# State products in rows of four, a contiguous tap table and whole-block turns in the S5 layer of a two-layer trunk on one Trainium2 core

## The chip, the core and the metric

The kernel runs on one core of one Trainium2 chip. A core has five engines that each work through their own queue of instructions in order: TensorE (PE: matmuls and transposes, with a separate queue PEld that loads the weights), VectorE (DVE), ScalarE (ACT), GpSimd (POOL) and SyncE (SP, which here starts all DMA transfers). They wait for each other only by semaphores. The metric is the device time of one execution in microseconds (us); of several executions the median counts, less is better.

## The reference

The model is a trunk of two layers on one sequence of 1024 steps with 1024 channels. Layer 0 is RWKV-7 time mixing, layer 1 an S5 state-space layer with a gated linear unit (GLU); each is followed by a squared-ReLU MLP, and every sub-layer by a layer norm of the scaled input plus the output. Only the S5 layer is changed. It has 64 groups of 16 channels; each group drives a diagonal complex state of 64 numbers.

```python
def s5_mix(x, a_re, a_im, log_dt, b_re, b_im, c_re, c_im, d_skip, w_glu):
    ...
    bbar_re, bbar_im = cmul(coef_re[..., None], coef_im[..., None], b_re, b_im)
    u = xf.reshape(bsz, n_chunks, CHUNK, SSM_GROUPS, SSM_GROUP).transpose(1, 2, 0, 3, 4)
    def chunk_step(h, u_c):
        bu_re = jnp.einsum('tbgc,gpc->tbgp', u_c, bbar_re)
        bu_im = jnp.einsum('tbgc,gpc->tbgp', u_c, bbar_im)
        pr, pi, sr, si = lax.associative_scan(combine, (a_ch_re, a_ch_im, bu_re, bu_im), axis=0)
        carry_re, carry_im = cmul(pr, pi, h_re[None], h_im[None])
        s_re, s_im = sr + carry_re, si + carry_im
        y = (jnp.einsum('tbgp,gcp->tbgc', s_re, cr_w) - jnp.einsum('tbgp,gcp->tbgc', s_im, ci_w))
        return (s_re[-1], s_im[-1]), y
    ...
    y = y.transpose(2, 0, 1, 3, 4).reshape(bsz, seq, d) + xf * d_skip
    y = jax.nn.gelu(y)
    z = y @ w_glu
    return z[..., :d] * jax.nn.sigmoid(z[..., d:])
```

## The kernel before

**Layout.** Activations lie with channels on the 128 partitions: `h[f]` is a tile of 128 channels (`f` from 0 to 7) by 512 steps, which is one half of the sequence. Half 0 is held in the tiles `hA`, half 1 in `hB`. The large products (MLP, GLU and the projections, called the bulk here) are made in three passes of rounded fp32 (`mm3`, all on line 188): every weight tile `wraw` is split into a rounded `whi` (ACT, L148) and a remainder `wlo` (DVE, L149), and one column of blocks sums into a PSUM bank `d`. `wload` (L169) is the DMA that fetches a weight tile. An instruction `L188 MATMUL d<-qbuf,whi` is one such bulk product.

**Order.** The tile framework schedules the instructions. Each has a rank; the bulk of the MLPs and the GLU has ranks from 200000 on, the S5 layer 99300 (half 0) and 99400 (half 1), its tables 99500, the layer norms 99000. A lower rank is taken first when its inputs are expected to be ready, and the bulk fills the places between; after this the order of each engine's queue is fixed in the program. So bulk products stand between the S5 layer's instructions on PE, and an S5 instruction that waits holds up the bulk behind it.

**PSUM.** Four pools share the eight banks: `d` (three, bulk), `l` (one, layer norms), `a` (two) and `c` (two).

**S5 tables** (L1105 to L1170, once). The layer works in blocks of `SL` = 8 steps, so 512 steps are `NSC` = 64 blocks. For each `f` (eight groups, two per `g2`: `par` is which of the two, in the partition halves) three tables are written to DRAM: `tB` (from inputs of a block to its states), `tC` (from states to outputs of a block) and `tT`, the taps, which take the inputs of a block straight to its outputs. For `tT` a product `pk` (L1151) gives the response to one input at distances of 0 to 7 steps, ACT copies it into `kpad` behind eight rows of zeros (cleared once by POOL), and two DMAs for each `f` (L1159) write eight shifted views of it as a block-Toeplitz table. In `kpad` and in `tT` the group `g` is the fastest index, so that the table of one group has every fourth element of a row.

**S5 layer**, once for each half (L1175 to L1268), with four rounds `f2` of two `f` each:

- Input: eight products with `ident` for each PSUM tile `pu1` turn 128 channels by every eighth step to 64 blocks by 128 channels (L154, L156: the upper partition half by a matmul, the lower by a transpose). ACT copies to `u1` (L1188). `pu2` (L1195) turns each group's part back, so that 8 steps x 16 channels lie on the partitions and the 64 blocks in the columns (`ug`, copied on L1197). `pbu` (L1206) multiplies with `tB`, and the result goes into the states `hb`.
- Scan: `advance` (L1216 to L1222) runs the recurrence over the 64 blocks, on DVE for groups of `g` 0 to 15 and on POOL for the rest, on DVE alone where the pieces are short.
- Output: for each `f2` the tables `tt` and `tcm` are loaded (L1240, L1242; tag `tab`, four buffers). For each `par` there is one PSUM bank `py`, into which 8 tap products (L1250, 128 partitions, `tt` streamed) and 16 state products (L1255, 64 partitions, `tcm` streamed) sum. ACT copies the bank to `y1` (L1257). Eight transposes for each `f` (`pyt`, L1263, in pool `a`) turn it back, DVE adds the direct path (`yg`, L1265, one buffer), ACT takes the GELU, and SP stores the row to DRAM as `s_y` (L1268), from where the GLU loads it as `yl` (L946).

## Time and profile before

| What | Value |
|---|---|
| median of 3 runs | 2742.12 us (2735.79 to 2742.68) |
| profiled execution, its time | 2746.6 us |
| span of its instructions | 2744.8 us |
| mean granted clock of TensorE | 0.961 |
| time busy: PE, PEld, DVE, ACT, POOL | 95%, 76%, 66%, 42%, 23% of the span |
| DMA | 345.90 MB, mean 126 GB/s |
| chain of work that ended last | PE 44%, DVE 4%, issue 3%, others 1% or less each |

The profile shows one execution. The span runs from the first to the last instruction; the execution's time is 1.8 us more. The times of the three runs lie within 6.9 us of each other, and the profiled execution lies 4.5 us above their median. A group such as `L1255 PE MATMUL py<-tcm,hb` is all instructions of one line and shape: their number, their busy time together, the mean duration of one, and the idle time before them. Durations of products that run beside each other overlap, so that a mean duration is not the time by which one of them delays the next.

### The profile page before, as it was taken

How to read it: one execution, taken by the hardware profiler on the slowest of the kernel's cores; microseconds unless marked ns; L12 is line 12 of the kernel's file. 1: busy time of each engine (PE TensorE's matmuls, PEld its weight loads, DVE VectorE, ACT ScalarE, POOL GpSimd, SP SyncE). 2: the span in 40 equal slices, each digit the busy share in tenths (PEclk: the TensorE clock that was granted, in tenths of full speed). 3: DMA queues.
4: the chain of work that ended last, by engine and by line, in shares of the span. 5: the costliest groups of instructions: out<-in, count | busy, mean ns of one | idle time of the engine just before them, and what ended most of it. 6: DMA issues, size and time to landing. Idle time of an engine off the chain costs nothing.

```text
span 2744.8 us, 43807 instructions
## 1 busy us (share of the span) xinstructions
PE 2598.4 (95%) x16582; PEld 2089.9 (76%) x16582; DVE 1813.3 (66%) x3191; ACT 1154.8 (42%) x2038; POOL 630.6 (23%) x515
## 2 busy tenths in 40 slices
PE   7999979989899999989999999999999999999997
PEld 5778757678677777767876788778778887788886
DVE  7477677577786867997567553674855546755556
ACT  7455574544543333353532332434223324433334
POOL 3121542432442122342122000120220101210101
PEclk9989979999899999999999999999999999999998
DMA  4765455564223334545333533233343322333333
GB/s 146 235 214 175 151 164 156 178 203 142 81 86 88 93 92 148 141 129 163 100 112 127 174 95 100 81 96 112 103 164 110 96 96 81 119 96 96 96 96 100
DMA packets 215058, 345.90 MB, mean 126 GB/s; under 512 B 21184, under 2 KB 75584, under 8 KB 214848
## 3 DMA queue, kind: packets, MB, share of 16 engines
q1 hardware_dynamic: 214848, 343.10, 40.5%
q8 instruction: 131, 2.15, 0.3%
q14 instruction: 79, 0.65, 0.1%
HBM read 279.06 MB, written 63.96 MB: 125 GB/s over the span
## 4 chain that ended last, share of the span: by engine, by line
PE 44%; DVE 4%; issue 3%; DMA 1%; POOL 1%; ACT 1%; ACTq 0%; SPq 0%; DVEq 0%; POOLq 0%
PE d L188 39%; PE py L1250 1%; PE py L1255 1%; DVE wlo L149 1%; DMA wraw<-in_mw_dram 1%; PE pu L154 1%; PE pbu L1206 1%; POOL rl L975 1%; DVE hA L991 0%; DMA s_y<-yg 0%; DVE t L1218 0%; DVE hB L991 0%; ACT whi L148 0%; DVE sq L876 0%; PE pu L1195 0%
## 5 line engine op out<-in xcount | busy, mean ns | idle before, releaser
L148 ACT CAST whi<-wraw 128x512 fp32r<-128x512 f32 x668 | 413.5, 620 | 929.1 <-PE d L188 623.2
L149 DVE TENSOR_TENSOR wlo<-wraw,whi 128x512 fp32r<-128x512 f32 x668 | 500.6, 750 | 426.8 <-ACT whi L148 404.3
L188 PE MATMUL d<-qbuf,whi 128*128 128x512 f32 (+1 forms) x2112 | 657.0, 394 | 23.8 <-DVE hA L991 12.8
L188 PEld LDWEIGHTS d<-qbuf,whi 128*128 128x128 f32 x2112 | 391.8, 191 | 120.0 <-DVE hA L991 17.8
L188 PE MATMUL d<-qbuf,wlo 128*128 128x512 f32 (+1 forms) x1056 | 411.9, 392 | 10.7 <-DVE wlo L149 10.4
L975 POOL TENSOR_TENSOR rl<-rl 128x512 f32<-128x512 f32 x128 | 157.2, 1228 | 1094.5 <-ACT rl L974 1094.5
L188 PE MATMUL d<-oAh,whi 128*128 128x512 f32 (+1 forms) x960 | 390.9, 411 | 15.5 <-ACT ev L418 6.3
L188 PE MATMUL d<-oAl,whi 128*128 128x512 f32 (+1 forms) x960 | 387.5, 405 | 3.0 <-DVE oAl L149 2.8
L188 PE MATMUL d<-oAh,wlo 128*128 128x512 f32 (+1 forms) x960 | 386.5, 405 | 2.4 <-DVE wlo L149 2.3
L188 PE MATMUL d<-oBh,whi 128*128 128x512 f32 x704 | 279.2, 397 | 0.0
L188 PE MATMUL d<-oBh,wlo 128*128 128x512 f32 x704 | 278.7, 396 | 0.2 <-DVE wlo L149 0.2
L188 PE MATMUL d<-oBl,whi 128*128 128x512 f32 x704 | 277.1, 394 | 0.0
L188 PEld LDWEIGHTS d<-qbuf,wlo 128*128 128x128 f32 x1056 | 201.7, 191 | 56.5 <-DVE wlo L149 14.5
L188 PEld LDWEIGHTS d<-oAh,whi 128*128 128x128 f32 (+1 forms) x960 | 185.9, 194 | 62.2 <-ACT ev L418 8.4
L188 PEld LDWEIGHTS d<-oAh,wlo 128*128 128x128 f32 (+1 forms) x960 | 185.8, 194 | 44.4 <-DVE wlo L149 3.2
L188 PEld LDWEIGHTS d<-oAl,whi 128*128 128x128 f32 (+1 forms) x960 | 185.6, 194 | 43.1 <-DVE oAl L149 5.2
L991 DVE TENSOR_TENSOR hB<-hB,d 128x512 f32<-128x512 f32 (+1 forms) x256 | 165.0, 650 | 71.2 <-PE d L188 68.0
L991 DVE TENSOR_TENSOR hA<-hA,d 128x512 f32<-128x512 f32 x240 | 162.1, 682 | 64.4 <-PE d L188 62.1
L188 PEld LDWEIGHTS d<-oBh,wlo 128*128 128x128 f32 x704 | 132.9, 189 | 32.4 <-issue 2.0
L188 PEld LDWEIGHTS d<-oBl,whi 128*128 128x128 f32 x704 | 133.1, 189 | 29.9 <-issue 0.7
L188 PEld LDWEIGHTS d<-oBh,whi 128*128 128x128 f32 x704 | 133.1, 189 | 29.0 <-issue 1.2
L149 DVE TENSOR_TENSOR qbuf<-rl,qbuf 128x512 fp32r<-128x512 f32 x128 | 95.0, 742 | 73.5 <-ACT qbuf L148 73.5
(374 smaller groups left out, 3804.8 us busy)
## 6 DMA issues: line engine op xcount, KB each, us to landing
wraw<-in_mw_dram SPq DMA_DIRECT2D x520, 256.0 KB, 2.7
wraw<-in_glu_dram SPq DMA_DIRECT2D x64, 256.0 KB, 2.7
low<-wlo SPq DMA_DIRECT2D x52, 256.0 KB, 2.6
wlo<-low SPq DMA_DIRECT2D x52, 256.0 KB, 3.6
wraw<-in_wk_dram SPq DMA_DIRECT2D x32, 256.0 KB, 3.5
wraw<-in_wr_dram SPq DMA_DIRECT2D x32, 256.0 KB, 3.9
wraw<-in_wv_dram SPq DMA_DIRECT2D x32, 256.0 KB, 4.3
yl<-s_y SPq DMA_DIRECT2D x32, 256.0 KB, 3.1
```

The costliest lines, as they stand in the source:

```text
L148: S.copy(hi, src)
L149: (e or V).tensor_sub(lo, src, hi.bitcast(F32))
L154: PE.matmul(out, x, idt, start=True, stop=True)
L188: bulk.append((PE.matmul(p, w, x, **kw).ins, x.shape[-1]))
L975: G.tensor_mul(r, r, r)
L991: V.tensor_add(z, z, p)
L1206: PE.matmul(p[qs, g2, ri], tb[:, g2, ri, qs], u[:, 2 * g2 + par], start=True, stop=True)
L1250: PE.matmul(p[64 * j : 64 * j + 64, g2], ug[f][:, 2 * g2 + par], tv[:, par, g2], start=g2 == 0, stop=False, skip_group_check=True)
L1255: PE.matmul(p[64 * j : 64 * j + 64, g2], hb[qs, 4 * f + g2, ri, 0:NSC], tcm[qs, g2, ri], start=False, stop=ri == 1, skip_group_check=True)
```

## The change

All of it is in the S5 layer and its tables. Line numbers of the kernel after are larger by 9 (bulk products: L188 becomes L197) to 19.

- **Input, turns of `h`.** In place of 64-row pieces of every eighth step, a whole 128x128 block is turned: all channels of one `f`, every fourth step (L1200). There are four for each `f`, all transposes. `u1` then has on its partitions 128 blocks of four steps.
- **Input, steps picked.** Blocks of four must be paired to blocks of eight. A new constant `sel` (made once, by one DVE copy of `ident` with even and odd columns apart) does it: `pu2` is now two products for each group (L1207), with the even and with the odd columns of `sel`, each into one half of the partitions.
- **Tap table.** `kpad`, `tT` and `tt` have the group ahead of the steps, so that one group's 128 numbers are contiguous. `kpad` is two tiles of four `f` each, of which POOL clears only the zeros; after every fourth `f`, 16 DMAs (two `par`, eight shifts) store four `f` at once, in place of two DMAs for each `f`.
- **Output.** Both banks `py` (one from pool `c`, one from pool `a`) are open at once. First all 16 tap products, then the 32 state products with the partition half (`par`, which is also the bank) as the innermost index and the column half (`j`) next. `inorder` ties each state product to the one ahead of it by a dependence without a semaphore, so that the scheduler keeps this order.
- **Turns of `y`.** `pyt` moves from pool `a` to the one bank of pool `l`.

```diff
+    sel = cp.tile([128, 2, 64], F32, name="sel")
+    V.tensor_copy(sel, ident.rearrange("p (n e) -> p e n", e=2))
...
+    def inorder(prods):
+
+        for x, y in zip(prods, prods[1:]):
+            tc.add_manual_dep(y.ins, x.ins.name, mybir.DependencyInfo(
+                mybir.DependencyClass.NoSync, mybir.DependencyReason.DATA), reason="order")
...
-    tT = dr.tile([KT, 128, 2, 512], F32, name="tT")
+    tT = dr.tile([128, 2, KT, 4, 128], F32, name="tT")
...
-        kpad = pp.tile([128, 16, 16, 4], F32, name="kpad")
-        G.memset(kpad, 0.0)
+        kpads = [pp.tile([128, TBF, 4, 16, 16], F32, name=f"kpad{j}") for j in range(KT // TBF)]
+        for kpad in kpads:
+            G.memset(kpad[:, :, :, 0:8], 0.0)
...
-                S.copy(kpad[ps_, 8:].rearrange("p t c g -> p g (t c)"), p[ps_])
-            tv = tT[f].rearrange("(s c) two n -> two c s n", c=16)
-            for par in range(2):
-                src = kpad[64 * par : 64 * par + 16, 1:9].rearrange("p t c g -> p (t c g)")
-                SP.dma_start(tv[par], bass.AP(src.tensor, src.offset, [src.ap[0], (64, SL), src.ap[1]]))
+                S.copy(kpad[ps_, f % TBF, :, 8:].rearrange("p g t c -> p g (t c)"), p[ps_])
+            if f % TBF == TBF - 1:
+                for par in range(2):
+                    for s in range(SL):
+                        SP.dma_start(
+                            tT[16 * s : 16 * s + 16, par, f - TBF + 1 : f + 1].rearrange("c f g n -> c (f g) n"),
+                            kpad[64 * par : 64 * par + 16, :, :, 1 + s : 9 + s].rearrange("c f g t e -> c (f g) (t e)"))
...
-            u1 = s5p.tile([128, 8, SL, 16], F32, tag="u1", name="u1", bufs=2)
-            for s2 in range(2):
+            u1 = s5p.tile([128, 2, 8, 4, 16], F32, tag="u1", name="u1", bufs=2)
+            for j in range(2):
                 p = pa.tile([128, 4, 128], F32, tag="a", name="pu1")
-                for j in range(2):
-                    src = h[2 * f2 + j].rearrange("p (c s) -> p c s", s=SL)
-                    for s in range(4):
-                        turn(p[64 * j : 64 * j + 64, s], src[:, :, SL - 1 - 4 * s2 - s], ident, j)
-                S.copy(u1[:, :, 4 * s2 : 4 * s2 + 4].rearrange("p g s c -> p s g c"),
-                       p.rearrange("p s (g c) -> p s g c", g=8))
+                src = h[2 * f2 + j].rearrange("p (m s) -> p s m", s=4)
+                for s in range(4):
+                    PE.transpose(p[:, s], src[:, 3 - s], ident)
+                S.copy(u1[:, j].rearrange("p g s c -> p s g c"), p.rearrange("p s (g c) -> p s g c", g=8))
...
                 for g in range(8):
-                    PE.transpose(p[:, g], u1[ps_, g].rearrange("p s c -> p (s c)"), ident[ps_, ps_])
+                    for e in range(2):
+                        PE.matmul(p[64 * (1 - e) : 64 * (1 - e) + 64, g], u1[:, j, g].rearrange("p s c -> p (s c)"),
+                                  sel[:, e], start=True, stop=True)
...
-                tabs.append((f, tt.rearrange("p two (n g) -> p two g n", g=4), tcm))
+                tabs.append((f, tt.rearrange("p two (g n) -> p two g n", g=4), tcm))
+            pp = [r.tile([128, HT], F32, tag=t, name="py").rearrange("p (g n) -> p g n", g=4)
+                  for r, t in ((pc, "c"), (pa, "a"))]
+            for g2 in range(4):
+                for par in range(2):
+                    for j, (f, tv, tcm) in enumerate(tabs):
+                        PE.matmul(pp[par][64 * j : 64 * j + 64, g2], ug[f][:, 2 * g2 + par], tv[:, par, g2],
+                                  start=g2 == 0, stop=False, skip_group_check=True)
+            prods = []
+            for g2 in range(4):
+                for ri in range(2):
+                    for j, (f, tv, tcm) in enumerate(tabs):
+                        for par in range(2):
+                            qs = slice(64 * par, 64 * par + 64)
+                            prods.append(PE.matmul(pp[par][64 * j : 64 * j + 64, g2], hb[qs, 4 * f + g2, ri, 0:NSC],
+                                                   tcm[qs, g2, ri], start=False, stop=ri == 1, skip_group_check=True))
+            inorder(prods)
             for par in range(2):
-                qs = slice(64 * par, 64 * par + 64)
-                p = pc.tile([128, HT], F32, tag="c", name="py").rearrange("p (g n) -> p g n", g=4)
...
-                S.copy(y1[:, :, :, par].rearrange("p t g c -> p g t c"), p.rearrange("p g (t c) -> p g t c", t=SL))
+                S.copy(y1[:, :, :, par].rearrange("p t g c -> p g t c"), pp[par].rearrange("p g (t c) -> p g t c", t=SL))
...
-                p = pa.tile([128, SL, NSC], F32, tag="a", name="pyt")
+                p = pl.tile([128, HT], F32, tag="l", name="pyt").rearrange("p (t n) -> p t n", t=SL)
```

Two places of PE's queue show what moved. The first is the turning of the input in half 0, round `f2` = 2, in the kernel before: L156 and L154 are turns of `hA` into a bank `pu1`, and the rows `d` are bulk products. Each row gives the line, the operation, output and inputs with the number of the buffer, the shape, and a count where instructions of one kind follow each other.

```order
L156 MATMUL pu1_13604<-ident_84,hA_7672 64x128 x4
L154 MATMUL pu1_13604<-ident_84,hA_7712 64x128 x4
L188 MATMUL d_14659<-oBh_12101,whi_14662 128x512
L188 MATMUL d_14659<-oBl_12102,whi_14662 128x512
L188 MATMUL d_14659<-oBh_12101,wlo_14663 128x512
L188 MATMUL d_14659<-oBh_12107,whi_14662 128x512
L188 MATMUL d_14659<-oBl_12108,whi_14662 128x512
L156 MATMUL pu1_13614<-ident_84,hA_7672 64x128 x4
L154 MATMUL pu1_13614<-ident_84,hA_7712 64x128 x4
```

The same place in the kernel after, from the second bank of that round on: L1200 is a whole-block turn, L1207 the picking of steps with `sel`.

```order
L1200 MATMUL pu1_13646<-ident_84,hA_7714 128x128 x4
L197 MATMUL d_14695<-qbuf_9518,whi_14691 128x512 x2
L197 MATMUL d_14695<-qbuf_9518,wlo_14692 128x512
L197 MATMUL d_14695<-qbuf_9518,whi_14691 128x512 x2
L197 MATMUL d_14695<-qbuf_9518,wlo_14692 128x512
L1207 MATMUL pu2_13652<-sel_112,u1_13639 64x64 x16
L1207 MATMUL pu2_13691<-sel_112,u1_13639 64x64 x16
```

A bank holds four turns of 128x128 from one `f` in place of eight of 64x128 from two, and the picking has 16 products of 64 columns for each `f` behind it, with other bulk products between.

The second place is the output stage of half 0, with the turns of `y` of round `f2` = 0 and the products of round 1. In the kernel before (names without the buffer's number, so that products into one bank stand in one row):

```order
L188 MATMUL d<-qbuf,wlo 128x512
L1250 MATMUL py<-tt,ug 64x128
L1263 MATMUL pyt<-ident,y_13883 128x64 x16
L1250 MATMUL py<-tt,ug 64x128 x7
L1255 MATMUL py<-tcm,hb 64x128 x16
L1250 MATMUL py<-tt,ug 64x128 x8
L1255 MATMUL py<-tcm,hb 64x128 x16
L188 MATMUL d<-oBh,whi 128x512
```

And in the kernel after, where L1282 is the turns of `y`, L1264 the tap products and L1272 the state products:

```order
L197 MATMUL d<-qbuf,wlo 128x512
L1282 MATMUL pyt<-ident,y_13935 128x64 x8
L1264 MATMUL py<-tt,ug 64x128 x14
L1272 MATMUL py<-tcm,hb 64x128 x13
L1282 MATMUL pyt<-ident,y_13935 128x64 x8
L1272 MATMUL py<-tcm,hb 64x128 x19
L1264 MATMUL py<-tt,ug 64x128 x2
L197 MATMUL d<-qbuf,whi 128x512 x2
```

The second eight turns of `y` now stand behind 14 tap and 13 state products, and behind the last state products stand the first two tap products of the next round, ahead of the bulk.

More of the change, by code (lines that the diff above doesn't have):

```diff
@@ L33 @@
 TB = 2
+TBF = 4
 LN8R = 400000
```

13 lines of the change are left out of this document (2 added, 11 removed).

## The prediction

> **What bounds the kernel now.** I read the page first, then the busy time by stage, then the timeline of TensorE inside the stages that the change touches.
>
> ```profile
> span 2744.8 us, 43807 instructions
> PE 2598.4 (95%) x16582; PEld 2089.9 (76%) x16582; DVE 1813.3 (66%) x3191; ACT 1154.8 (42%) x2038; POOL 630.6 (23%) x515
> ...
> L149 DVE TENSOR_TENSOR wlo<-wraw,whi 128x512 fp32r<-128x512 f32 x668 | 500.6, 750 | 426.8 <-ACT whi L148 404.3
> ```
>
> TensorE (PE) is busy for 95% of the span, so its time counts, but only where it is also the last to wait. The busy time by stretch shows that (columns: stretch, its length, busy time and instruction count of PE, PEld, DVE, ACT, POOL, granted clock, DMA share, GB/s).
>
> ```profile
> 1327.00:1400.00 73.00, 73.00 (x577) 59.23 (x577) 33.80 (x52) 32.07 (x55) 4.18 (x4) 1.00 0.33 105
> 1400.00:1480.00 80.00, 72.35 (x354) 55.24 (x351) 68.18 (x115) 21.23 (x36) 25.95 (x14) 0.97 0.32 99
> 1480.00:1542.00 62.00, 62.00 (x534) 46.95 (x533) 28.82 (x39) 21.88 (x36) 8.68 (x5) 0.99 0.63 219
> ...
> 1940.00:2010.00 70.00, 62.67 (x257) 47.86 (x254) 65.90 (x112) 18.82 (x32) 18.08 (x10) 0.96 0.27 87
> 2010.00:2071.00 61.00, 61.00 (x532) 46.76 (x532) 27.66 (x36) 20.41 (x35) 7.49 (x5) 0.99 0.55 190
> 1072.00:1270.00 198.00, 178.08 (x931) 135.86 (x931) 184.06 (x355) 85.85 (x136) 70.50 (x50) 0.95 0.54 149
> ```
>
> The S5 layer has three stages in each half: the input is turned (1327 to 1400 in half 0), the scan runs on DVE (1400 to 1480), the outputs are made (1480 to 1542). In the first and the third PE is busy for 73.00 of 73 and 62.00 of 62 us, and DVE for less than half: a microsecond of PE saved there is saved. In the scan, and while the tables are made (1072 to 1270), DVE is nearly full (68.18 of 80, 184.06 of 198) and PE has idle time already.
>
> **The change part by part.** Counts first. An fp32 product shows as two records, a transpose as one; the rows are of half 0 for hA (hB has the same again) and of both halves for the others.
>
> ```profile
> L1250 PE MATMUL py<-tt,ug 128*64 128x128 f32 x256 | 40.4, 408 | 0.0
> ...
> L1255 PE MATMUL py<-tcm,hb 64*64 64x128 f32 x512 | 32.5, 275 | 0.0
> ...
> L154 PE MATMUL pu<-ident,hA 128*64 128x128 f32 x64 | 9.5, 294 | 0.0
> ...
> L1195 PE MATMUL pu<-ident,u 64*128 64x64 f32 x128 | 8.1, 229 | 0.0
> ...
> L156 PE MATMUL pu<-ident,hA 128*64 128x128 f32 x32 | 4.6, 272 | 0.0
> ```
>
> Records overlap, so I take their price from start to start in the timeline of PE (columns: start, length of the run, what, how many). First the turning stage:
>
> ```profile
> 1327.37 1.03 PE L156 MATMUL pu<-ident,hA 128*64 128x128 f32 x8
> 1328.34 2.19 PE L154 MATMUL pu<-ident,hA 128*64 128x128 f32 x16
> 1330.46 0.73 PE L188 MATMUL d<-qbuf,whi 128*128 128x512 f32 x2
> ...
> 1337.99 1.01 PE L1195 MATMUL pu<-ident,u 64*128 64x64 f32 x16
> 1338.94 0.50 PE L188 MATMUL d<-oBh,wlo 128*128 128x512 f32 x1
> ...
> 1343.73 2.09 PE L1206 MATMUL pbu<-ug,tb 128*64 128x64 f32 x64
> 1345.74 0.50 PE L188 MATMUL d<-oBl,whi 128*128 128x512 f32 x1
> ```
>
> *Turning h.* Eight L156 records take 0.97 us to the next start, 0.121 each; sixteen L154 records take 2.12, 0.133 each. So 64 x 0.121 + 128 x 0.133 = 24.8 us. After it there are 64 transposes of whole 128x128 blocks, all of the one-record kind; at 0.121 they cost 7.7. **Gain 17.1.** Their weights, 128 columns taken from every fourth element of h, are not in this trace. L156 reads every eighth and L154, at 0.133, the same; twice L156's price (0.242) is my upper end, 7.7 us more. I take 0.121, since it is the nearest row.
>
> The SBUF — State Buffer page of the Trainium skill (Specifications (TRN2)) says that a read at full bandwidth needs two hits in each 16-byte line and that each new line pays; every fourth fp32 is a new line each time, so by it the new turns pay and the forecast would be some 7 us later. L156, whose step also leaves the line each time, ran at 0.121 us, so I don't count it.
>
> *Picking the steps.* 128 transposes at 0.95 / 16 = 0.059 cost 7.6 us. They become 256 products with `sel`, of the form of L1206 (128 rows, 64 columns of weights, 64 columns streamed, column halves in turn): 2.01 / 64 = 0.0314 a record, 512 records, 16.1 us. **Loss 8.5.**
>
> Now the output stage, one f2 of it:
>
> ```profile
> 1489.03 0.65 PE L1250 MATMUL py<-tt,ug 128*64 128x128 f32 x2
> 1489.60 1.01 PE L1263 MATMUL pyt<-ident,y 64*128 64x64 f32 x16
> 1490.55 2.01 PE L1250 MATMUL py<-tt,ug 128*64 128x128 f32 x14
> 1492.49 1.96 PE L1255 MATMUL py<-tcm,hb 64*64 64x128 f32 x32
> 1494.38 2.01 PE L1250 MATMUL py<-tt,ug 128*64 128x128 f32 x16
> 1496.33 1.96 PE L1255 MATMUL py<-tcm,hb 64*64 64x128 f32 x32
> 1498.22 0.51 PE L188 MATMUL d<-oBh,whi 128*128 128x512 f32 x1
> ```
>
> *Tap products.* 32 L1250 records take 0.57 + 1.94 + 1.95 = 4.46 us, 0.139 each, 35.6 for 256. State products stream 128 columns as well and take 1.89 / 32 = 0.059. The difference is the streamed table, which steps over four elements; another product with 128 contiguous columns, pk, runs as the state products do:
>
> ```profile
> 1125.14 1.71 PE L1151 MATMUL pk<-ca,bb 64*16 64x128 f32 x28
> ```
>
> 28 records in 1.71 us, 0.061 with the last one's drain. At 0.059 the 256 tap records cost 15.1. **Gain 20.5.** If the step was not the cause, the gain is 0; nothing else differs from L1206 but the width.
>
> *State products.* 512 x 0.059 = 30.2 us, two side by side (two column halves). Four in a row use both row halves too, into two banks. The trace has this once by chance, where the first half's 32 records of a run of 64 end and the second's begin. Instructions in flight at four moments, by short stretches on that line (PE's count is the first in brackets):
>
> ```profile
> 1482.30:1482.31 0.01, 0.01 (x5) 0.01 (x2) 1.00 1.05 410
> ...
> 1483.06:1483.07 0.01, 0.01 (x10) 0.01 (x4) 1.00 0.00 0
> 1484.00:1484.01 0.01, 0.01 (x5) 0.01 (x2) 1.00 0.00 0
> ```
>
> Ten records are in flight instead of five: four run at once at the pace of two. So 30.2 becomes 15.1: **gain 15.1.** The turns of y are cut into 16 pieces in place of 8 and the products are cut at them; at about 0.1 us a piece (an estimate from the gaps between the rows above) that is a loss of 0.8.
>
> On PE: 17.1 - 8.5 + 20.5 + 15.1 - 0.8 = 43 us.
>
> *What comes late next.* Three rows on the y's, from DVE's timeline, and two landings:
>
> ```profile
> 1494.35 1.19 DVE L1265 SCALAR_TENSOR_TENSOR yg<-hA,pv,pyt 128x512 f32<-128x512 f32 x1 [2.82 <-DMA s_y<-yg]
> 1504.58 1.19 DVE L1265 SCALAR_TENSOR_TENSOR yg<-hA,pv,pyt 128x512 f32<-128x512 f32 x1 [2.17 <-PE pyt L1263]
> 1508.62 1.16 DVE L1265 SCALAR_TENSOR_TENSOR yg<-hA,pv,pyt 128x512 f32<-128x512 f32 x1 [0.86 <-DMA s_y<-yg]
> ```
>
> ```profile
> tt<-tT SPq DMA_DIRECT2D x16, 512.0 KB, 4.2
> ...
> s_y<-yg SPq DMA_DIRECT2D x16, 256.0 KB, 2.8
> ```
>
> One f2 took PE 9.2 us of products plus 21 bulk products at 0.23, 14 us. It becomes 1.0 (turns) + 1.9 + 1.9 + 0.5 and 18 bulk at 0.23, about 9.4. But yg has one buffer: the next y waits for the store of the last (4.0 us from 1504.58 to 1508.62, more where the store is slow), two of them 8 to 12 us. pyt moves into the ring "l", which has one bank: the second turn waits for DVE to finish the first y, and PE, which is in order, with all bulk behind it, waits too. Also two tap products of the next f2 now stand before the bulk (below the 19 state products). Their table's buffer is freed by the tap products of this f2, 32 state products and a turn earlier, 2.5 us, and the load takes 4.2: a wait of about 2 us at four places. I give back 12 us in all (8 of it by these four waits, the rest by the turns); the bounds are 0, if stores land in 2 us and waits overlap, and 6 f2 x 3.3 = 20.
>
> In the scans the order has 28 more bulk products than before (288 and 280 for 270 each). DVE is full there, and each twelve bring one wlo (0.75 us) and about one add more: I count 3 us back, 0 to 5.
>
> At nothing: in the table stage `kpad` is cleared and stored in two blocks of 16 DMAs (POOL has 128 of 198 us free; ACT's sixteen copies of 1.07 us get cheaper, off the path). Each block keeps SP for about 16 x 0.36 = 6 us without a weight load, and SP has slack there, since it waits for DVE:
>
> ```profile
> SPq L169 <- DVE wlo L149: 100.0, 48, 7.9
> ```
>
> If that cover is gone, two blocks cost up to 12. The copy of `sel` at the start is below 0.3.
>
> **The sum** is 43 - 12 - 3 = 28 us off the profiled execution (span 2744.8, run 2746.6), so 2718.6; the runs' median, 2742.12, lies 4.5 lower: **2714**.
>
> **The rivals.** (1) *Nothing is given back*: y's stores land in 2 us and no table is late. 2742 - 43 = 2699. For it: DVE is under half busy there. Against it: the wait for s_y is in the rows. (2) *The output stage keeps its length*, held by tables, stores and the single bank: then only the turning stage (8.6) and the tap products ahead of the scan (a quarter of 20.5, 5) are won, 2728. For it: DMA is at 0.63 there and must carry the same bytes in two thirds of the time. (3) *Four in a row run two at a time*: the change doesn't do what it says, 15 us less, and the waits shrink by about 5 since PE comes later: 2724. For it: each product is two records for one part of the array, and if a record that waits for its part stops all behind it, no more than two overlap. Against it: the ten in flight. The page TensorE: Matmul & The Clock Gate of the Trainium skill (Part 3, The mechanism) calls the matmuls' start strictly first in, first out, which would give this rival; the trace disagrees with it at 1483.06. (4) *Slower by the clock*:
>
> ```profile
> 1470.00:1475.00 5.00, 1.93 (x6) 0.97 (x6) 5.00 (x6) 1.05 (x2) 1.15 (x1) 0.99 0.11 13
> 1475.00:1481.00 6.00, 5.20 (x12) 3.80 (x12) 6.00 (x8) 1.24 (x2) 4.01 (x3) 0.50 0.20 77
> ```
>
> After 5 us with PE busy for 1.93, the clock was granted at 0.50 for 6 us, which costs 3. If the new waits (16 turns of y and 4 tables, 2 us each) trip it too, each costs 5: nine use the gain up, eleven of the twenty give 2742 - 43 + 55 = 2754. Against it: waits of 2 us leave PE mostly busy in any 5.
>
> **How the numbers follow.** Chances: the forecast 0.60 (its own range 2704 to 2725), (1) 0.14, (2) 0.14, (3) 0.08, (4) 0.04. The range of 2696 to 2734 takes in all but (4) and the outer ends of (1) and (2), which move by the bounds above (the turns up to 7.7 dearer, the return of waits from 0 to 20), about 0.8. 0.3% is 8.2 us, about what a measurement of this kernel can tell from no change: faster than 2734 is all of the forecast, (1) and (3) and some four in ten of (2), 0.88; the rest of (2) lies within, 0.08; slower is (4), 0.04.
>
> **What would show it.** Right: tap records in pairs at 0.109 us from pair to pair, state records four to 0.109 us, 64 whole turns at 0.12, the step products at 0.031; the output stages at about 46 us each with PE idle for some 6 in each, before pyt and the first tap products. Wrong: state records still at 0.059; whole turns above 0.2; output stages at 60 us; half-clock rows in the output stages; or PE idle in the table stage by 10 us more, beside the two blocks of stores.

## The result and the profile after

The change made the kernel slower: 2754.41 us median of 9 runs (2744.84 to 2760.1) beside 2737.66 us of 9 runs of the kernel before (2726.34 to 2749.15); the ratio is 1.0056, 95% interval 1.0038 to 1.0074. That is some 15 us in the wrong direction; the forecast had been 28 us less. (The ratio of the run called sel alone below leaves out one of its twelve executions, which took 5681.63 us.) The page of the profiled execution, in the rows that answer to those of before (the split of the weights, L148 and L149 before, is L151 and L152 here):

```profile
span 2758.1 us, 44305 instructions
PE 2574.1 (93%) x16838; PEld 2080.2 (75%) x16838; DVE 1824.3 (66%) x3192; ACT 1146.2 (42%) x2038; POOL 627.2 (23%) x516
...
L152 DVE TENSOR_TENSOR wlo<-wraw,whi 128x512 fp32r<-128x512 f32 x668 | 505.2, 757 | 408.9 <-ACT whi L151 390.2
```

PE is busy for 24 us less and the span is 13 us longer, so PE waits for some 38 us more. Where, is best seen between marks that stand at the same work in both kernels. Both issue the same 9338 bulk records (products into `d`) in nearly the same order, so I take the times at which the 3181st, 3841st, 4561st, 5881st and 6481st begin. They bound the table stage, the S5 layer of half 0, a stretch without S5 work, and the S5 layer of half 1 (us, each from one profiled execution; the first mark is at 1071.6 us before and 1081.7 after):

| | tables | S5, half 0 | between | S5, half 1 | the four |
|---|---|---|---|---|---|
| before | 214.3 | 250.3 | 310.3 | 218.5 | 993.4 |
| after | 238.8 | 234.8 | 311.1 | 212.2 | 997.0 |

The S5 layer gained 21.8 us and **the table stage lost 24.5**. The busy time of the table stage, from its first mark to its last, before and then after (columns as in the prediction):

```profile
1071.60:1285.90 214.30, 194.38 (x1005) 149.37 (x1004) 194.69 (x372) 89.39 (x142) 72.82 (x52) 0.95 0.56 157
```

```profile
1081.70:1320.50 238.80, 197.04 (x1005) 150.91 (x1004) 196.31 (x372) 81.78 (x142) 73.31 (x53) 0.90 0.51 141
```

The work is the same (1005 products, 372 and 372 DVE instructions, DVE 195 and 196 us); the stage has only become longer around it, at a lower granted clock. What stood in the way is in SP's timeline: start, length, how many. First the change, with the weight loads (L172) and the table load `bc` (L1121) around its first block, then three of the eight pairs of stores of before:

```profile
1181.06 0.33 SPq L172 DMA_DIRECT2D wraw<-in_mw_dram  x1
1181.44 19.54 SPq L1170 DMA_DIRECT2D tT<-kpad  x16
...
1204.41 0.82 SPq L1121 DMA_DIRECT2D bc<-in_s5bc_dram  x1
1205.29 11.48 SPq L172 DMA_DIRECT2D wraw<-in_mw_dram  x4
...
1285.55 20.28 SPq L1170 DMA_DIRECT2D tT<-kpad  x16
```

```profile
1128.61 0.90 SPq L1159 DMA_DIRECT2D tT<-kpad  x2
...
1158.20 2.37 SPq L1159 DMA_DIRECT2D tT<-kpad  x2
...
1268.48 0.86 SPq L1159 DMA_DIRECT2D tT<-kpad  x2
```

A block of 16 stores of the tap table holds SP for 20 us, 1.25 us a store on the mean, and no weight load leaves in that time; the next one starts 23.8 and 21.7 us after the block's start. The stretches behind the two blocks, and what PE waited for from the first mark to 1345 us (us, times, longest; 26.6 us of it lie in the table stage, where the kernel before has no such wait over 0.15 us):

```profile
1201.00:1209.00 8.00, 0.00 (x0) 0.00 (x0) 0.00 (x0) 1.08 (x2) 0.00 (x0) 0.74 0.89 226
1290.00:1306.00 16.00, 8.26 (x37) 6.46 (x35) 4.23 (x7) 0.68 (x2) 0.00 (x0) 0.83 0.76 99
1306.00:1322.00 16.00, 7.54 (x24) 5.77 (x24) 5.29 (x9) 1.78 (x3) 2.56 (x2) 0.64 0.77 245
```

```profile
PE d L197 <- ACT whi L151: 27.5, 4, 15.3
```

For 8 us behind the first block no matmul ran; behind the second PE stood for half of 32 us, and the clock fell to 0.64. The chain goes from the store over SP's queue to the weight load, `whi`, and the bulk product. The tables' own transfers were held too: DVE stood for 8.4 us until 1209.04 for the load `bc` that SP could start only at 1204.41.

In the S5 layer the trace shows most of what was forecast. The timeline of PE, from a turn of `h` to the picking of steps and then one output round:

```profile
1364.64 1.12 PE L1200 MATMUL pu<-ident,hA 128*128 128x128 f32 x8
...
1371.86 0.86 PE L1207 MATMUL pu<-sel,u 128*64 128x64 f32 x22
...
1498.60 1.98 PE L1272 MATMUL py<-tcm,hb 64*64 64x128 f32 x64
1500.51 0.50 PE L197 MATMUL d<-oBh,whi 128*128 128x512 f32 x1
...
1506.21 0.71 PE L1282 MATMUL pyt<-ident,y 64*128 64x64 f32 x8
1506.84 1.96 PE L1264 MATMUL py<-tt,ug 128*64 128x128 f32 x28
1508.73 1.08 PE L1272 MATMUL py<-tcm,hb 64*64 64x128 f32 x26
1509.75 0.71 PE L1282 MATMUL pyt<-ident,y 64*128 64x64 f32 x8
1510.39 1.32 PE L1272 MATMUL py<-tcm,hb 64*64 64x128 f32 x38
1513.14 0.65 PE L1264 MATMUL py<-tt,ug 128*64 128x128 f32 x4 [1.43 <-DMA tt<-tT]
```

64 state records take 1.91 us, 0.030 each, where before 32 took 1.89: four in a row do run at once. 28 tap records take 1.89, 0.068 each in place of 0.139. At 1513.14 stands the forecast wait for a tap table, 1.43 us.

### The profile page after: what moved, and what is told of

Read it like the earlier page. It is cut to its first block, busy times and chain, and to the rows that moved or that the text cites. A ratio compares the mean times of both kernels' runs of the same rounds, so it can differ in the third digit from the quotient of the medians.

```text
span 2758.1 us, 44305 instructions
## 1 busy us (share of the span) xinstructions
PE 2574.1 (93%) x16838; PEld 2080.2 (75%) x16838; DVE 1824.3 (66%) x3192; ACT 1146.2 (42%) x2038; POOL 627.2 (23%) x516
## 4 chain that ended last, share of the span: by engine, by line
PE 63%; DVE 16%; DMA 8%; ACT 5%; issue 4%; POOL 2%; SPq 2%; ACTq 0%; DVEq 0%; POOLq 0%
PE d L197 54%; DVE wlo L152 3%; PE pA L605 2%; SPq L1170 1%; DMA wraw<-in_wr_dram 1%; ACT whi L151 1%; DMA wraw<-in_mw_dram 1%; DMA tt<-tT 1%; DMA s_r<-ev 1%; DVE t L1231 1%; DMA ldsg<-s_sg 1%; DVE hA L1000 1%; PE pu L1207 1%; PE pbu L1219 1%; DVE qbuf L152 1%
## 5 line engine op out<-in xcount | busy, mean ns | idle before, releaser
L151 ACT CAST whi<-wraw 128x512 fp32r<-128x512 f32 x668 | 413.8, 620 | 963.6 <-PE d L197 635.7
L152 DVE TENSOR_TENSOR wlo<-wraw,whi 128x512 fp32r<-128x512 f32 x668 | 505.2, 757 | 408.9 <-ACT whi L151 390.2
L197 PE MATMUL d<-qbuf,whi 128*128 128x512 f32 (+1 forms) x2112 | 660.8, 396 | 41.1 <-ACT whi L151 16.3
L197 PEld LDWEIGHTS d<-qbuf,whi 128*128 128x128 f32 x2112 | 395.2, 192 | 136.2 <-DVE hA L1000 22.4
L197 PE MATMUL d<-qbuf,wlo 128*128 128x512 f32 (+1 forms) x1056 | 413.4, 394 | 9.2 <-DVE wlo L152 9.0
L197 PE MATMUL d<-oAh,whi 128*128 128x512 f32 (+1 forms) x960 | 393.0, 412 | 28.6 <-ACT whi L151 10.6
L984 POOL TENSOR_TENSOR rl<-rl 128x512 f32<-128x512 f32 x128 | 148.9, 1163 | 1084.2 <-ACT rl L983 1084.1
L197 PE MATMUL d<-oAl,whi 128*128 128x512 f32 (+1 forms) x960 | 388.9, 406 | 2.5 <-DVE oAl L152 2.4
L197 PE MATMUL d<-oAh,wlo 128*128 128x512 f32 (+1 forms) x960 | 387.1, 406 | 1.3 <-DVE wlo L152 1.3
L197 PE MATMUL d<-oBh,whi 128*128 128x512 f32 x704 | 279.4, 397 | 3.2 <-DVE hB L1000 1.9
L197 PE MATMUL d<-oBh,wlo 128*128 128x512 f32 x704 | 278.3, 396 | 0.0
L197 PE MATMUL d<-oBl,whi 128*128 128x512 f32 x704 | 277.0, 393 | 0.0
L197 PEld LDWEIGHTS d<-qbuf,wlo 128*128 128x128 f32 x1056 | 202.8, 192 | 55.5 <-DVE wlo L152 13.1
L197 PEld LDWEIGHTS d<-oAh,whi 128*128 128x128 f32 (+1 forms) x960 | 186.7, 195 | 73.8 <-ACT whi L151 11.1
L197 PEld LDWEIGHTS d<-oAl,whi 128*128 128x128 f32 (+1 forms) x960 | 187.0, 195 | 43.0 <-DVE oAl L152 4.6
L197 PEld LDWEIGHTS d<-oAh,wlo 128*128 128x128 f32 (+1 forms) x960 | 186.6, 195 | 43.4 <-DVE wlo L152 2.1
L197 PEld LDWEIGHTS d<-oBh,whi 128*128 128x128 f32 x704 | 133.1, 189 | 31.9 <-issue 3.1
L197 PEld LDWEIGHTS d<-oBh,wlo 128*128 128x128 f32 x704 | 132.7, 189 | 32.0 <-issue 1.8
L197 PEld LDWEIGHTS d<-oBl,whi 128*128 128x128 f32 x704 | 132.9, 189 | 29.9 <-issue 1.0
L152 DVE TENSOR_TENSOR qbuf<-rl,qbuf 128x512 fp32r<-128x512 f32 x128 | 99.9, 780 | 66.3 <-ACT qbuf L151 66.1
```

The source lines that it names most:

```text
L151: S.copy(hi, src)
L152: (e or V).tensor_sub(lo, src, hi.bitcast(F32))
L197: bulk.append((PE.matmul(p, w, x, **kw).ins, x.shape[-1]))
L984: G.tensor_mul(r, r, r)
```

## The experiments

The table gives for each run the ratio to before with its interval, and the same four stretches from its one profiled execution. One execution says little about a few us: sel alone, which changes next to nothing, differs from before by 6 us in the sum, and it is the timed ratio that decides.

| run | ratio (95%) | tables | S5, 0 | S5, 1 | the four |
|---|---|---|---|---|---|
| the change | 1.0056 (1.0038 to 1.0074) | 238.8 | 234.8 | 212.2 | 997.0 |
| old tap table | 0.9976 (0.9961 to 0.9991) | 213.6 | 244.3 | 219.1 | 987.4 |
| new tap table alone | 1.0066 (1.0049 to 1.0083) | 235.8 | 244.0 | 211.2 | 1002.6 |
| sel alone | 1.0012 (0.9998 to 1.0025) | 210.9 | 248.8 | 217.7 | 987.3 |
| 16 small stores after each f | 1.0066 (1.0054 to 1.0078) | 237.6 | 240.9 | 216.8 | 1005.5 |
| stores from POOL | 1.0071 (1.0052 to 1.0090) | 227.9 | 251.7 | 213.7 | 1004.2 |
| stores from ACT | 1.0047 (1.0033 to 1.0060) | 230.7 | 245.5 | 215.6 | 1002.3 |
| tap tables loaded first | 1.0047 (1.0034 to 1.0060) | 234.8 | 243.7 | 209.3 | 999.3 |
| two in a row | 1.0067 (1.0054 to 1.0080) | 235.6 | 240.6 | 215.3 | 1003.9 |
| output stage alone | 1.0011 (0.9998 to 1.0025) | 213.4 | 248.1 | 216.0 | 989.9 |
| input stage alone | 0.9993 (0.9979 to 1.0006) | 210.8 | 244.4 | 215.6 | 983.1 |
| old tap table, loaded first | 0.9967 (0.9949 to 0.9984) | 212.7 | 242.2 | 208.3 | 979.7 |
| 8 stores after each f | 0.9969 (0.9953 to 0.9984) | 213.0 | 245.8 | 214.1 | 983.9 |
| 8 stores, loaded first | 0.9964 (0.9952 to 0.9976) | 210.2 | 241.7 | 207.8 | 975.8 |
| the same, two banks for the turns | 0.9980 (0.9966 to 0.9993) | 213.2 | 245.4 | 215.9 | 985.6 |

**Old tap table.** All of the change but the tap table, which is that of before.

```diff
-                        SP.dma_start(
-                            tT[16 * s : 16 * s + 16, par, f - TBF + 1 : f + 1].rearrange("c f g n -> c (f g) n"),
-                            kpad[64 * par : 64 * par + 16, :, :, 1 + s : 9 + s].rearrange("c f g t e -> c (f g) (t e)"))
+                SP.dma_start(tv[par], bass.AP(src.tensor, src.offset, [src.ap[0], (64, SL), src.ap[1]]))
...
-                tabs.append((f, tt.rearrange("p two (g n) -> p two g n", g=4), tcm))
+                tabs.append((f, tt.rearrange("p two (n g) -> p two g n", g=4), tcm))
```

> The change with the tap table of before (two stores of 2 KB runs for each f, strided taps), all else of the change kept. Theory A, the two blocks of 16 stores hold SP for 20 us each and cost 25 us in the table stage: that stage is as long as before (from the first table products to the first turn of h within 5 us), the taps cost 17 us more than in the change, and the whole comes out 8 to 20 us under the change, from 0.993 to 1.002 of before. Theory B, the loss is from the first 1070 us, which the change does not mean to touch (10 us later in its one profile): the same 10 us are there again and the ratio to before is 1.002 to 1.006. Theory C, the loss is in the S5 stages themselves (waits for tables, the single bank, the clock): the ratio stays above 1.004, with the table stage as long as in the change or not.

Measured: 0.9976, about 7 us faster than before and 22 under the change. The table stage is back at 213.6 us. So the loss is in the new table (theory A), not in the turns or the order of products. The first mark is at 1071.9 us, as before (1071.6).

**New tap table alone**, in the kernel before.

```diff
-        kpad = pp.tile([128, 16, 16, 4], F32, name="kpad")
+        kpads = [pp.tile([128, TBF, 4, 16, 16], F32, name=f"kpad{j}") for j in range(KT // TBF)]
...
+            if f % TBF == TBF - 1:
+                for par in range(2):
+                    for s in range(SL):
+                        SP.dma_start(
...
```

> The kernel before with the new tap table alone: blocks of 16 stores, contiguous taps, the turns and the order of products as before. Theory A: the table stage is 25 us longer, the taps 17 us shorter, so 1.001 to 1.005 of before, and the stores of one block take about 20 us on SP. Theory C: the table stage is not much longer than before, and the kernel is faster than before by 10 to 17 us (0.994 to 0.996).

```profile
1171.31 19.31 SPq L1162 DMA_DIRECT2D tT<-kpad  x16
```

Measured: 1.0066. The block holds SP for 19.3 us here too, and the stage is 21.5 us longer. The taps cost PE 18.0 us less (20.6 in place of 38.6), as expected, but the two S5 halves are only 6.3 and 7.3 us shorter. The loss is larger than theory A had it (1.001 to 1.005).

**sel alone.** The early constant, read by nothing.

```diff
+    sel = cp.tile([128, 2, 64], F32, name="sel")
+    V.tensor_copy(sel, ident.rearrange("p (n e) -> p e n", e=2))
```

> The kernel before with the constant sel made at the start (512 bytes a partition more, every later tile moved by as much; sel is read by nothing). Theory B, something of the change makes the first 1070 us longer by 10 us: this is the only part of the change that stands there, so the ratio is 1.003 to 1.005 and the part up to the tables is 8 us longer. Theory A and C: no difference, 0.998 to 1.002; the first 1070 us vary from run to run by several us.

Measured: 1.0012, not told from no change; its first mark is at 1072.3 us. The 10 us by which the profiled execution of the change was late at its first mark were that execution's own: other kernels with the same beginning reached it at 1062.5 to 1074.7. Theory B falls.

**16 small stores after each f.**

```diff
-TBF = 4
+TBF = 1
```

> The change with the stores of the tap table spread: after each f 16 stores of 32 KB, in place of 16 of 128 KB after each fourth. Bytes and runs are the same. Theory A1, it is the block that hurts, since weight loads stand behind 20 us of stores on SP: each group holds SP for about 5 us, the table stage is 15 to 25 us shorter than in the change, and the whole is 0.994 to 0.999 of before. Theory A2, each store costs SP a fixed time of over a microsecond whatever its size: 128 stores hold SP longer than 32, and the table stage is longer still, 1.01 and up. Theory A3, it is the time of the DMA engines for runs of 512 bytes: the table stage stays 10 to 25 us longer than before, wherever the stores stand.

```profile
1130.85 0.33 SPq L172 DMA_DIRECT2D wraw<-in_wo_dram  x1
1131.23 7.54 SPq L1170 DMA_DIRECT2D tT<-kpad  x16
...
1143.04 1.53 SPq L172 DMA_DIRECT2D wraw<-in_wo_dram  x2
```

Measured: 1.0066, and 237.6 us in the table stage. A store of a quarter of the bytes still takes SP 0.46 us, so that 128 of them hold it for some 60 us in all, more than the 40 of the blocks. At each group, 11 to 19 us pass between two weight loads. Spreading alone doesn't help when the number of stores grows with it. A1 had the hold right in kind (7.5, not 5 us), but not what a hold of that length costs. A2 is out, with 0.46 us a store. A3, the runs of 512 bytes, forecast just this result and is not ruled out here; the run with 8 stores below does that.

**Stores from POOL, stores from ACT.** The same blocks, started by another engine.

```diff
-                        SP.dma_start(
+                        G.dma_start(
```

> The change with the 32 stores of the tap table started by POOL in place of SP; the same bytes, runs and blocks. Theory S, the loss is SP's: weight loads stand in SP's queue behind stores that take 1.25 us each. Then nothing holds SP, the table stage is back within 8 us of before (214 us between the same two bulk products, 239 in the change), and the whole is 0.990 to 0.995 of before, which is the 22 us that the S5 stages gained. Theory D, the loss is the DMA engines': runs of 512 bytes keep them busy whoever starts them, and weight loads land late all the same; the table stage stays 12 us or more above before, and the whole is 0.999 to 1.005. POOL is busy for 70 of 198 us there; if a store holds it for over a microsecond, its products of the tables come late, and that too would show as a longer stage, with waits for POOL.

> The same with ACT in place of POOL. Theory S: SP is free, but ACT makes every whi that TensorE waits for, so that whatever a store takes on the queue that starts it now stands ahead of whi; if it is 1.25 us as on SP, two blocks of 20 us cost as much as in the change (table stage 232 to 245 us, ratio 1.003 to 1.008). Theory D: as with POOL, the stage is longer by 12 us or more, whoever starts the stores. If a store's 1.25 us are not the queue's but room in a ring that only SP's loads fill, ACT is held for a few us only and the stage is back at 214 to 222 us (0.990 to 0.996).

The DMA list of the first (KB each, us from issue to landing), and the timeline of ACT in the second:

```profile
tT<-kpad POOLq DMA_DIRECT2D x32, 128.0 KB, 10.5
```

```profile
1166.16 21.00 ACTq L1170 DMA_DIRECT2D tT<-kpad  x15
1187.20 1.07 ACT L1180 COPY bs<-pb 128x512 f32<-128x512 f32 x2 [20.71 <-DMA tT<-kpad]
```

Measured: 1.0071 and 1.0047; the table stage is 13.6 and 16.4 us longer than before, in place of 24.5. So theory S alone is not enough. From POOL, SP holds no store and the weight loads leave, but those beside a block land after 5.7 to 14.7 us in place of the usual 2.8: the block's 2 MB take 24 to 27 us until the last store has landed, whichever of the three engines starts them. (POOL itself is held for 15 us by each block.) From ACT the loads land in 3.0 to 4.5 us, but ACT is held for 21 us and makes no `whi`. Both theories are half right: 2 MB at once stand in the way, by holding the engine that starts them, and from POOL by slowing the loads beside them. (In both runs the S5 layer of half 0 is longer than in the change as well; I have no cause for that beyond the other schedule that follows.)

**8 stores after each f.** One store for each group and `par`, with all eight shifts in it: half as many as above, for one `f` at a time.

```diff
-            if f % TBF == TBF - 1:
-                for par in range(2):
-                    for s in range(SL):
...
+            for par in range(2):
+                for g in range(4):
+                    src = kpad[64 * par : 64 * par + 16, f % TBF, g, 1:9].rearrange("p t e -> p (t e)")
+                    SP.dma_start(tv[par, g], bass.AP(src.tensor, src.offset, [src.ap[0], (16, SL), src.ap[1]]))
```

> The change with the stores of the tap table cut another way: after each f 8 stores of 64 KB (one for each group, all eight shifts in it), 64 stores in all, the same bytes and 512-byte runs. With 16 stores of 32 KB after each f SP was held for 7.5 us and no weight load left for 13 us each time. If a store has a price on SP of about 0.46 us, the hold is now 3.7 to 4.5 us each time, the table stage is 224 to 230 us between the same two bulk products (214 before, 238 in the change), and the whole is 0.998 to 1.002 of before. If the price goes with the number of runs (1024 after each f in both), the hold stays at 7 to 8 us and the ratio at 1.005 to 1.008.

```profile
1125.11 4.11 SPq L1171 DMA_DIRECT2D tT<-kpad  x8
...
1132.53 1.90 SPq L172 DMA_DIRECT2D wraw<-in_wo_dram  x2
...
1144.25 4.08 SPq L1171 DMA_DIRECT2D tT<-kpad  x8
```

Measured: 0.9969, faster than before, where the change is slower. The bytes and the 512-byte runs are those of the change. SP is held for 3.9 to 5.5 us eight times, each group has landed 6.3 to 7.4 us after its start (6 us before), and the table stage is 213.0 us, better than the 224 to 230 expected: a hold of this length costs nothing that shows. This settles the table stage: it is not the runs of 512 bytes, but how long what stands behind a group of stores has to wait. From a group's start to the next weight load 2 to 7 us pass in the kernel before, 4 to 10 with 8 stores, 8 to 12 with 16 small ones, and 22 and 24 in the change. How long the loaded weights last can be read from the change: from the start of a block PE made 43 and 53 more bulk products, 11.5 and 12.4 us of its time, before it stood still. A weight load needs 2.8 us to land and 1.4 for its split, so that it has to start within some 8 us (an estimate from these numbers): 8 stores are about within it, 16 small ones at its edge or past it, and a block far outside. Why 16 small ones lose as much as the blocks is argued from these numbers and not shown further.

**Tap tables loaded first**, in the change: both `tt` ahead of both `tcm` in SP's queue.

```diff
-            for f in (2 * f2, 2 * f2 + 1):
-                tt = s5p.tile([128, 2, 512], F32, tag="tab", name="tt", bufs=4)
...
+            for f, tt in zip(fs, tts):
+                SP.dma_start(tt.rearrange("p two (g n) -> p two g n", g=4), tT[:, :, f])
...
+            for f, tcm in zip(fs, tcms):
                 SP.dma_start(tcm, tC[f])
```

> The change with both tap tables of a round loaded ahead of both state tables (in the change the second tap table stands in SP's queue behind the first state table, whose buffer comes free only after the state products). TensorE waits 8.2 us for tap tables in the two output stages of the change. If the queue's order is the cause, that wait falls to 3 us or less and the whole is 3 to 8 us under the change (1.002 to 1.005 of before); if the load itself is too slow (4.7 us to landing), the wait stays at 6 us or more and the time is that of the change. The table stage stays as long as in the change.

Measured: 1.0047; its interval lies largely over that of the change, so no difference can be told. The wait for tap tables falls from 8.2 to 3.3 us (all in half 0), but 8.1 us before the turns of `y` take its place.

**Two in a row.** The 32 state products in the order of before.

```diff
-            for g2 in range(4):
-                for ri in range(2):
-                    for j, (f, tv, tcm) in enumerate(tabs):
-                        for par in range(2):
+            for par in range(2):
+                for g2 in range(4):
+                    for ri in range(2):
+                        for j, (f, tv, tcm) in enumerate(tabs):
```

> The change with the 32 state products of a round in the order of before, one bank after the other (16 and 16), so that only the two column halves alternate; both banks still open together, the order still fixed. If four in a row is what makes them quick (17.3 us for both halves in the change, 31.3 before), they take 30 to 31 us again and the whole is 8 to 14 us longer than the change, since some of the loss is taken out of waits for tables: 1.009 to 1.011 of before. If the two open banks or the fixed order were enough, the records stay at 17 us and the time is that of the change.

```profile
1480.45 3.34 PE L1272 MATMUL py<-tcm,hb 64*64 64x128 f32 x64
```

64 records take 3.34 us here and 1.98 in the change; in the two halves together 27.5 us against 17.3. It is the order that makes them quick. The ratio, 1.0067, lies above the change's but short of the 1.009 to 1.011 expected, and the intervals overlap: 10 us of PE in the output stage are hardly seen in the time.

**Output stage alone, input stage alone**, each in the kernel before (the first has also the old input, the second the old output and both the old tap table).

```diff
+            inorder(prods)
...
+                p = pl.tile([128, HT], F32, tag="l", name="pyt").rearrange("p (t n) -> p t n", t=SL)
```

> The kernel before with the output stage of the change alone (state products four in a row into two banks, turns of y in the bank of pool l); the input turns and the tap table are those of before. TensorE's own time falls by 14 us for the states and rises by 2.7 for the turns of y, as the change showed. If that much arrives, the ratio is 0.995 to 0.997; if the waits it brings in the output stage (tap tables 4 us a half, the clock after them) eat it, 0.998 to 1.001. The first turning stage and the table stage are as before.

```diff
+                for s in range(4):
+                    PE.transpose(p[:, s], src[:, 3 - s], ident)
```

> The kernel before with the input stage of the change alone (whole 128x128 turns, steps picked with sel); output stage and tap table as before. TensorE's own time falls by 18.7 us for the turns and rises by 9.1 for the picking. The input stage has no other bound in the trace of before (PE busy for all of it), so 6 to 10 us should arrive: 0.9965 to 0.998. If the scan, which DVE bounds, only starts earlier and is longer for it, less than 4 us arrive: 0.9985 to 1.0005.

Measured: 1.0011 and 0.9993; neither is told from no change. In the output stage alone the states fall from 31.3 to 17.8 us of PE's time, and PE's waits in the S5 layer rise from 15.9 to 25.9 us. What PE waited for from the scan on, in half 0:

```profile
PE d L195 <- DVE hB L998: 6.2, 6, 1.5
PE py L1258 <- DMA tt<-tT: 3.9, 1, 3.9
PE d L195 <- ACT rl L981: 2.5, 2, 1.6
```

**Both repairs, and two banks for the turns.** 8 stores after each `f` together with the tap tables first; old tap table with the tap tables first; and the first of these with every second turn of `y` in a bank of pool `a`.

```diff
-                p = pl.tile([128, HT], F32, tag="l", name="pyt").rearrange("p (t n) -> p t n", t=SL)
+                p = (pa.tile([128, HT], F32, tag="a", name="pyt") if j else pl.tile([128, HT], F32, tag="l", name="pyt")).rearrange("p (t n) -> p t n", t=SL)
```

> The change with the tap table of before, and both tap tables of a round loaded ahead of both state tables. Against the same without the new order of loads (0.9976 of before) it should lose the wait for tap tables in the output stages (0.7 and 4.0 us there) and some half-clock time behind it: 0.994 to 0.997. If the order of loads doesn't matter, 0.997 to 0.999.

> The change with both repairs: 8 stores of the tap table after each f (one for each group), and both tap tables of a round loaded ahead of both state tables. With the first alone (0.9969 of before) TensorE still waits 12.4 us for tap tables in the two output stages. If that wait is the queue's order, it falls to 4 us or less, half-clock time behind it falls too, and the whole is 0.992 to 0.996 of before. If the load cannot be earlier since its buffer comes free too late, the wait and the ratio (0.996 to 0.998) stay.

> The same, and the second turn of y of each round in a bank of pool a in place of the one bank of pool l. If the single bank holds TensorE (3 to 4 us before the turns of y in each output stage where the tables came early), that wait goes and the whole is 2 to 6 us shorter than without it. If the one buffer yg and its store are the limit, the wait moves to the next turn and nothing is gained.

Measured: 0.9967, 0.9964 and 0.9980. The version with both repairs has the lowest ratio here (2730.7 us beside 2739.14 of before in the same session), though the intervals of the first two and of the 8 stores alone lie over each other; it lies in the range forecast for the case that the waits for tap tables stay, although they went. Those waits fall from 12.4 to 1.1 us, and two others come up in their place, seen from the input stage to the outputs of half 0:

```profile
PE d L197 <- DVE hB L1000: 8.7, 6, 3.4
PE pyt L1280 <- DVE yg L1282: 2.8, 1, 2.8
```

With a second bank the wait before the turns goes from 8.3 to 2.2 us in both halves, but the tables are late again (10.8 us), and nothing is gained. With the old, strided tap table the taps cost PE 13.6 us more in the S5 layer than with the contiguous one (35.7 against 22.1), PE waits 11.4 us less (19.6 against 31.0), and the ratio is the same. So, once the tables come early, the contiguous taps buy mostly idle time.

## Why the prediction was wrong

**The step that failed** is the one that costed an edit at nothing: each block "keeps SP for about 16 x 0.36 = 6 us without a weight load, and SP has slack there", at most 12 us for both. The blocks held SP for 19.5 and 20.3 us and the stage lost 24.5. Two things were wrong in it. The price was that of stores that come in pairs: 0.36 us is the median of the 16 in the kernel before. In the first block the first three took 0.43, 0.44 and 0.61 us and the other thirteen 1.33 on the mean (1.39 in the second block). The trace of before had one sign of it, the pair at 1158.20, whose second store took 1.26 us. And the cover was read from SP's waits for DVE (100.0 us in 48 pieces), which are slack only piece by piece, of 7.9 us at the longest; none is there for a hold of 20 us in one piece. The number that should have been compared is how long the loaded weights last, about 12 us with the landing and the split of the next load included. The prediction had priced up to 12 us for a lost cover, but left them out of its range; the last of its signs of being wrong is the one that came: PE is idle for 41.8 us in the table stage in place of 19.9.

**The terms on PE** stood. Start to start, without idle time, in both halves:

| us | before | after | change | forecast |
|---|---|---|---|---|
| turns of h | 26.5 | 7.8 | -18.7 | -17.1 |
| steps picked | 7.6 | 16.7 | +9.1 | +8.5 |
| tap products | 38.6 | 21.0 | -17.6 | -20.5 |
| state products | 31.3 | 17.3 | -14.0 | -15.1 |
| turns of y | 7.6 | 10.3 | +2.7 | +0.8 |
| together | | | -38.5 | -43.4 |

The whole turns with columns from every fourth element cost no more than the old ones, so the upper end of that term was not needed, and the rule on 16-byte lines quoted from the page SBUF — State Buffer of the Trainium skill was not seen in these turns' time. The streamed table is another matter: contiguous, the same products took a little over half the time, by the layout alone (20.6 us in the run with only the new table, 37.7 in the change with the old one). Four in a row do not run two at a time (rival 3): two in a row, in the same kernel, took 27.5 us in place of 17.3. At 1498.60 four records start within 0.02 us, in order, and run side by side, so products that start in order are not thereby limited to two.

**What was given back** in the S5 layer was forecast at 15 us and is 17 in this execution: 13.5 us more idle time of PE (8.2 of it for tap tables, where the prediction had 8 at four places) and 3.4 us more in the bulk products, with a lower granted clock in half 1 (0.96 in place of 0.98). But the layer's net gain of 21.8 us in the change flatters it. With the table stage repaired, the same S5 code gains 8.9 us there (245.8 and 214.1 against 250.3 and 218.5), and with the tables loaded first 19.3, of which 5.8 go in the stretch between. So a second term was too small: in the run with 8 stores the terms on PE come to 38.0 us, and 29 of them are given back, not 15 (20.7 us more idle time of PE and 8.4 us more in the bulk products, at a lower clock). Even without the loss in the table stage some 9 us arrive of the 28, and the timed ratio of that run, 0.9969, says the same. A part of the change's short half 0 seems to be work of DVE that caught up while PE stood still for the stores; I infer this from the comparison and did not test it.

**The rivals.** Rival 2, that the output stage keeps its length, came nearest to what the change does: from the first state product to the last turn of `y` the change takes 51.7 and 55.4 us, the kernel before 52.7 in both halves (with 109 and 103 bulk products in between in place of 79). Its output stage alone brings nothing, and one wait takes the place of another (tap tables, then the turns' bank and `yg`, then tap tables again). With 8 stores and the tables loaded first the stage does come down to 47.0 and 45.8 us, about the 46 forecast, and yet the time hardly moves. I gave rival 2 a chance of 0.14. Rival 4, slower by the clock, named the sign with the wrong place: the clock did fall (0.95 to 0.90 in the table stage), mostly behind waits for weights, not behind the new waits for `y`. That its 2754 us are the measured 2754.41 is luck.

**What stays open.** The four stretches explain 4 us of the change's 15 by the profile of before, 10 by the profile of sel alone; the rest is not located, and one execution of each kernel does not resolve it. That the same blocks started by POOL or ACT lose time in the table stage too, 13.6 and 16.4 us beside SP's 24.5, was shown; what limits a block to 2 MB in 24 us was not tried.

## What to carry to other kernels

A DMA issue that is free one at a time is not free sixteen at a time: before several stores are gathered into a block, compare the length of the whole hold, at the pace of a full queue, with the time that the loads behind it are ahead, and prefer few stores often (here 8 at a time). An engine with much slack in total may have none in one piece. And work taken from an engine that is busy for the whole of a short stage comes back as waiting unless the loads and buffers that stage feeds on become earlier by as much.

## What was not expected of the hardware

- A store on SP's queue mostly takes about 0.42 us whether it has 64 or 128 runs of 512 bytes, and 1.36 us on the mean in a row of stores with 256 runs each, from the fourth on. Each of these had started when three or four such stores, 768 to 1024 runs, were still under way; whether that is a limit was not tested.
- Stores started by POOL let SP's queue go on and slow down what it carries: weight loads beside them landed in 5.7 to 14.7 us in place of 2.8.
